# 64 unused bytes ahead of three groups of SBUF tiles in a one-core encoder block

## The chip, the cores and the metric

The kernel runs on one core of a Trainium2 chip. The metric is the device time of one execution in microseconds (us); before the change it is 1456.45 us, the median of three runs (1454.12, 1456.45 and 1457.32). Profiles are of one execution each; a profile's span runs from its first to its last instruction. TensorE does the matrix products, VectorE (DVE) and ScalarE (ACT) the elementwise work, GpSimd (POOL) some of it and a few transfers, SyncE (SP) issues most transfers.

## The reference, cut to what matters

One layer of a block over 1024 tokens of width 1024, all in float32. Two branches share one input projection:

```python
h = rms_norm(h_res, norm_w[layer])
z = jnp.einsum('bsd,dc->bsc', h, w_in[layer].astype(f32))
qkv_a, g_a, q_b, zf_fwd, zf_bwd, i_b, g_b, zgate_a, zgate_b = jnp.split(z, split_points, axis=-1)
...
q = rms_norm(qkv_a[:, :, g, 0], q_norm_w[layer, g])
k = rms_norm(qkv_a[:, :, g, 1], k_norm_w[layer, g])
...
y_a = jnp.einsum('bsc,cd->bsd', o_a.reshape(B, S, ATTN_WIDTH) * jax.nn.silu(g_a), w_proj_a[layer].astype(f32))
...
y_b = jnp.einsum('bsc,cd->bsd', o_b.reshape(B, S, HG_WIDTH), w_proj_b[layer].astype(f32))
merged = jax.nn.sigmoid(zgate_a) * y_a + jax.nn.sigmoid(zgate_b) * y_b
h_res = h_res + jnp.einsum('bsd,de->bse', merged, w_out[layer].astype(f32))
```

Branch (A) is dilated window attention in three groups of eight heads, branch (B) a gated linear recurrence (HGRN2) in both directions. Three places matter here: the input projection and its norm (the opening), the norms of q and k over the 64 columns of each head (the norm sums), and the last three products y_a, y_b and the output (the closing stage).

## The kernel before

**Products of split pairs.** [...] To keep precision, each operand is split into a high part and a low part, for weights `whi` and `wlo`, and each product is made of three matmuls: high by high, high by low, low by high. Nearly all such matmuls are of 128 by 128 (the stationary operand, loaded first) by 512 columns (the moving operand). In the names of the profile, `gp<-xh,whi` is a matmul into a tile `gp` with `xh` moving and `whi` stationary.

**The order of the work** is made while the program is built. The class `Plan` (from line 116) keeps a model of each engine's time, and `Builder.task` and `tick` (from line 247) put the work of ACT, DVE, POOL and SP between the products according to it. The model knows no addresses. Each engine then works through its own list in order.

**The stages on TensorE**, by the profile's times:

- *The opening* (from 6 us): the values of the first attention group are computed from `uhi`, `ulo` (the input times the norm's weight, split) before the norm is known (`u_products`, line 944), and those of the second group partly so (`u_group`, line 1031). The u tiles are stationary there, in part of it; the other part, and the third group's value pass (line 1107), uses the normalised input hT as stationary operand, in four quarters `hh00`, `hh01`, `hh10`, `hh11` and their low parts (line 727). The names leave the digits out: `hh`, `hl`. The quarter for tokens 512 and up and the first half of the width, `hh10` and `hl10`, lies in a pool of its own (line 721).
- *The blocks* (about 142 to 682 us): attention's q and k and other columns of the projection (`run_quads`, line 448), with a scheme of seven products in place of eight. Banks are called `qA`, `qE`, `qC`; the moving operands are hT and its sums `S0` to `S3`, the weights are stationary. For the norms of q and k, the squares are summed over each head by a matmul with a matrix of ones, `headones`, as stationary operand and the squares' parts `nhi`, `nlo` as moving ones (`head_sums`, line 1142). There are 48 such pairs of matmuls, called `nss`, put in between the others. The weights of this stage are loaded into the ring `qraw`; the finished q and k leave from the ring `ny`.
- *Attention, merge and HGRN2* (about 682 to 1248 us). In the merge, bursts of three matmuls called `al` spread the heads' weights (line 1532), with `sel` stationary and `alB` moving.
- *The closing stage* (from 1248 us to the end): first y_a (bank `gp`, moving `xh`, `xl`: the split output of attention), then y_b by seven products (banks `sA`, `sE`; moving `xh`, `xl`), then the output by seven products, in which `xh` and `xl` are stationary and the weights move (`seven`, line 2141). Weights come through the ring `eraw` and, for y_a, through `raw`; the gates come through the ring `sg`; evacuations go to `acc`, `ma` and `sg`.

**Where tiles lie.** A pool is a stretch of each partition of SBUF, and tiles lie in it one behind the other in the order in which they are first asked for. Pools that are closed make room for later ones. Three pools matter: `pre` (line 739, the opening), `blocks` (line 1095, in `blocks_start`) and `end` (line 1990, in `end_start`). Two earlier pools already hold unused tiles (`tinyPad`, line 631, and `pad`, line 708). The start of each tile, modulo 256 bytes, in the built program of before:

| tiles | pool | begins at, modulo 256 |
|---|---|---|
| raw, whi, wlo, stage | wts, stg | 224 |
| hh, hl, quarters 00, 01, 11; S0 to S3; hbh, hbl; sel, alB | hT, sums, h10b, merge | 224 |
| hh10, hl10 | h10 | 160 |
| uhi, ulo, x, v | pre | 160 |
| headones, qraw, spare, ny, nhi, nlo | blocks | 160 |
| acc, xh, xl, sg | end | 160 |
| eraw, ma, ob | endo | 224 |

Slices that the matmuls take of a tile begin at multiples of 512 bytes in it, so the start of each operand has its tile's remainder.

Of the kernel before, what the change touches and what calls it, by code (L numbers as in the profile page):

```python
# [8 lines left out]
F32 = mybir.dt.float32  # L9
# [613 lines left out]
def hybrid_block(ctx, tc, a, out):  # L623
# [115 lines left out]
    pre = pctx.enter_context(tc.tile_pool(name="pre", bufs=1))  # L739
# [2 lines left out]
    ones = pre.tile([128, 128], F32, name="ones")  # L742
    g_.memset(ones, 1.0)
    A0, A1 = 64, 576
    uhi = pre.tile([128, 8, 512], F32R, name="uhi")
    ulo = pre.tile([128, 8, 512], F32R, name="ulo")
    v_ring = b.ring(pre, "v", 10, [128, 512])
# [340 lines left out]
    def blocks_start():  # L1088

        if "p" in blk or blk["n"] < 16:  # L1090
            return
        b.low = "pool"
        tctx.close()
        a21.close()
        blk["p"] = p = gctx.enter_context(tc.tile_pool(name="blocks", bufs=1))
        blk["raw"] = b.ring(p, "qraw", QRAW, [128, 512])
        blk["spare"] = b.ring(p, "spare", SPARE, [128, 512])
        blk["ones"] = p.tile([128, 128], F32R, name="headones")
        blk["lo"] = b.ring(p, "nlo", 2, [128, 512], F32R)
        blk["hi"] = b.ring(p, "nhi", 2, [128, 512], F32R)  # L1100
        blk["y"] = b.ring(p, "ny", 4, [128, 512])
        a_.preload_act_table_set("natural_log_exp_and_others")
        v_.tensor_copy(blk["ones"].rearrange("p (j c) -> p j c", j=2),
                       half_ones[:, :, None].to_broadcast([128, 2, 64]))
        b.start_quads(blk["raw"])

    for g in (1, 2):
        if g == 2:
            grs = [tok_group(pos, 128 * i, evac_v(g, 128 * i), last=(k >= 6))
                   for k, i in enumerate((4, 5, 6, 7, 0, 1, 2, 3))]  # L1110
        for k, gr in enumerate(grs[:6]):
            if g == 1 and k < 5:
                continue
            b.run_unit([gr])
            if g == 2 and k >= 3:
                blocks_start()
        b.run_unit(grs[6:])
        pos += 8
    b.until(lambda: blocks_start() or "p" in blk)


# [866 lines left out]
    def end_start():  # L1988
        bctx.close()
        ectx["ep"] = ep = ctx.enter_context(tc.tile_pool(name="end", bufs=1))  # L1990
        ectx["acc"] = b.ring(ep, "acc", 10, [128, 512])
        ectx["xh"] = b.ring(ep, "xh", 12, [128, 512], F32R)
        ectx["xl"] = b.ring(ep, "xl", 12, [128, 512], F32R)
        ectx["sg"] = b.ring(ep, "sg", 5, [128, 512])
        for k in range(8):
            b.task("sp", [oaD], lambda k=k: load_oa(k % 4, k // 4), 4, ectx["acc"].soon)

    def load_oa(j, half):
        t = ectx["acc"].get()
        s_.dma_start(t, oaD[j, half])  # L2000
        b.task("act", [t], lambda: (OA.__setitem__((j, half), split_x(t)), ectx["acc"].done(t)), 4)
# [11 lines left out]
    for j in range(LATE, 8):  # L2013
        for half in range(2):
            b.run_unit([T_group(pos, half, evac_sg(1, j, half), half == 1)])
            if not ectx and all(st.get("f", 0) == 2 for st in H.values()):
                end_start()
        pos += 2
    b.drain()
    if not ectx:  # L2020
        end_start()
        b.drain()
# [7 lines left out]
    ep, acc, sgr = ectx["ep"], ectx["acc"], ectx["sg"]  # L2030
# [377 lines left out]
def _build(arrays):  # L2408
    import concourse.bacc as _bacc
    nc = _bacc.Bacc("TRN2", target_bir_lowering=False, num_devices=1)  # L2410
    args = {n: nc.dram_tensor(f"in_{n}_dram", v.shape, mybir.dt.from_np(v.dtype), kind="ExternalInput").ap()
            for n, v in arrays.items()}
    out = nc.dram_tensor("out_0_dram", (S, D), F32, kind="ExternalOutput").ap()
    with tile.TileContext(nc) as tc:
        hybrid_block(tc, args, out)
    return nc
# [9 lines left out]
```

## Time and profile before

| | |
|---|---|
| time, median of three runs | 1456.45 us |
| the three runs | 1454.12, 1456.45, 1457.32 us |
| span of the profiled execution | 1453.1 us |
| TensorE busy | 1444.3 us, 99% |
| DVE, ACT, POOL busy | 67%, 62%, 23% |
| instructions in the profile | 22946 |

The profiled execution's own time is not given apart from its span; the three timed runs lie 1.0 to 4.2 us above that span. [...] The chain of waits names, for each stretch of time, what the end of the program waited for.

### The profile page before, as it was taken

To read this page: it belongs to the slowest core of one execution; us is meant where nothing else is said; L and a number is where in the kernel's file an instruction comes from. 1 tells how busy PE (TensorE), PEld (TensorE's weight loads), DVE (VectorE), ACT (ScalarE), POOL (GpSimd) and SP (SyncE) were. 2 spreads that over 40 slices of the span, in tenths; PEclk is the share of its full clock that TensorE was granted. 3 is DMA by queue.
4 is the path that set the end of the run, shared out by engine and by line. 5 is a ranking of instruction groups with operands and counts; after the bars stand their busy time and mean duration, and the time that the engine had idled before them with its cause. 6 is when DMAs were issued, how large, how long until landed. Compare 5 with 4: busy or idle time off the path is not lost.

```text
span 1453.1 us, 22946 instructions
## 1 busy us (share of the span) xinstructions
PE 1444.3 (99%) x7930; PEld 1197.2 (82%) x7930; DVE 968.1 (67%) x1901; ACT 894.9 (62%) x1900; POOL 340.3 (23%) x356
## 2 busy tenths in 40 slices
PE   9999999999999999999999999999999999999998
PEld 8788888888888888888888778888888888788887
DVE  6673678678685788331564649487878786358973
ACT  7743767466565676443688852497777784558461
POOL 0102434464523433333002000031222221001011
PEclk9999999999999999999999999999999999999999
DMA  7746567777643334324848449354444453778665
GB/s 238 181 143 196 165 195 162 192 153 170 148 123 102 98 105 114 111 102 144 280 144 282 151 118 326 123 141 105 126 109 125 110 138 75 225 240 220 181 154 136
DMA packets 194992, 230.75 MB, mean 159 GB/s; under 512 B 46083, under 2 KB 118043, under 8 KB 194364
## 3 DMA queue, kind: packets, MB, share of 16 engines
q1 hardware_dynamic: 180188, 203.93, 45.0%
q0 software_dynamic: 13824, 25.17, 11.7%
q8 instruction: 62, 1.02, 0.3%
q14 instruction: 54, 0.44, 0.1%
q10 hardware_dynamic: 864, 0.19, 0.1%
HBM read 169.29 MB, written 81.43 MB: 173 GB/s over the span
## 4 chain that ended last, share of the span: by engine, by line
PE 90%; DVE 5%; ACT 3%; DMA 1%; issue 1%; SPq 0%; POOL 0%; ACTq 0%; DVEq 0%
PE gp L58 25%; PE qA L58 20%; PE qE L58 10%; PE sA L58 6%; PE qC L58 5%; PE sE L58 5%; PE u L58 3%; PE o L58 3%; PE oB L58 3%; PE pT L58 2%; PE sc L58 2%; PE nss L58 2%; DVE Bc L58 1%; PE U L58 1%; DVE S L58 1%
## 5 line engine op out<-in xcount | busy, mean ns | idle before, releaser
L58 POOL TENSOR_TENSOR wlo<-qraw,whi 128x512 fp32r<-128x512 f32 x135 | 194.3, 1444 | 381.8 <-ACT whi L58 293.8
L58 ACT ACTIVATE whi<-qraw 128x512 fp32r<-128x512 f32 x189 | 117.7, 626 | 100.8 <-DVE qraw L58 43.1
L58 DVE TENSOR_TENSOR qraw<-qraw,qraw 128x512 f32<-128x512 f32 x108 | 100.0, 927 | 39.0 <-POOL wlo L58 28.0
L58 PE MATMUL gp<-hh,whi 128*128 128x512 f32 x264 | 109.7, 416 | 0.0
L58 PE MATMUL gp<-hh,wlo 128*128 128x512 f32 x264 | 103.6, 393 | 0.0
L58 PE MATMUL gp<-hl,whi 128*128 128x512 f32 x264 | 103.0, 390 | 0.0
L58 ACT ACTIVATE as<-as,neg 128x192 f32<-128x192 f32 (+2 forms) x192 | 83.8, 442 | 16.8 <-DVE neg L58 16.7
L58 ACT ACTIVATE whi<-raw 128x512 fp32r<-128x512 f32 x92 | 57.6, 627 | 43.8 <-PE gp L58 18.7
L58 PE MATMUL qA<-hh,whi 128*128 128x512 f32 x216 | 84.4, 391 | 0.0
L58 PE MATMUL qA<-hh,wlo 128*128 128x512 f32 x216 | 84.3, 390 | 0.0
L58 DVE CUSTOM_DVE_ANT_0 as<-sc,abias 128x192 f32<-128x192 f32 (+2 forms) x192 | 56.0, 348 | 42.4 <-PE sc L58 27.1
L58 PE MATMUL qA<-hl,whi 128*128 128x512 f32 x216 | 84.0, 389 | 0.0
L58 POOL COPY mm<-Bc 128x8 f32<-128x8 f32 x64 | 32.2, 534 | 205.6 <-DVE Bc L58 123.6
L58 PE MATMUL gp<-whi,hh 128*128 128x512 f32 x192 | 78.6, 409 | 0.0
L58 PE MATMUL gp<-wlo,hh 128*128 128x512 f32 x192 | 75.2, 391 | 0.4 <-DVE wlo L58 0.4
L58 PE MATMUL gp<-whi,hl 128*128 128x512 f32 x192 | 75.0, 391 | 0.0
L58 DVE TENSOR_TENSOR wlo<-qraw,whi 128x512 fp32r<-128x512 f32 x54 | 37.3, 691 | 49.6 <-ACT whi L58 49.6
L58 DVE SCALAR_TENSOR_TENSOR ny<-ny,spare 128x512 f32<-128x512 f32 x48 | 67.4, 1405 | 1.6
L58 ACT ACTIVATE ny<-ny 128x512 f32<-128x512 f32 x96 | 60.8, 633 | 4.0 <-DVE ny L58 0.8
L58 PEld LDWEIGHTS gp<-hh,wlo 128*128 128x128 f32 x264 | 49.5, 188 | 11.0
L58 POOL DMA_DIRECT2D wlo<-in_w_in_dram x36 | 31.5, 875 | 113.6 <-ACT wlo L58 97.8
L58 PEld LDWEIGHTS gp<-hh,whi 128*128 128x128 f32 x264 | 49.8, 188 | 8.3
(306 smaller groups left out, 4208.2 us busy)
## 6 DMA issues: line engine op xcount, KB each, us to landing
qraw<-in_w_in_dram SPq DMA_DIRECT2D x108, 256.0 KB, 3.8
raw<-in_w_in_dram SPq DMA_DIRECT2D x84, 256.0 KB, 3.7
qkD<-ny SPq DMA_DIRECT2D x48, 256.0 KB, 2.8
wlo<-in_w_in_dram POOLq DMA_DIRECT2D x36, 256.0 KB, 4.4
sg<-sgD SPq DMA_DIRECT2D x32, 256.0 KB, 3.7
eraw<-wsD SPq DMA_DIRECT2D x32, 256.0 KB, 3.3
sgD<-stage SPq DMA_DIRECT2D x26, 256.0 KB, 2.7
ak<-qkD SPq DMA_DIRECT2D x6, 1024.0 KB, 6.6
```

What stands on the lines that cost most here:

```text
L58: got = f(*args, **kw)
```

## The change

Each of the three pools gets one more tile of 128 partitions by 16 float32 values, 64 bytes per partition, that nothing writes or reads. It is asked for ahead of the others (in `pre` behind `warm` and `ones`), so that all tiles behind it lie 64 bytes further.

```diff
     A0, A1 = 64, 576
+    pre.tile([128, 16], F32, name="prePad")
     uhi = pre.tile([128, 8, 512], F32R, name="uhi")
...
         blk["p"] = p = gctx.enter_context(tc.tile_pool(name="blocks", bufs=1))
+        p.tile([128, 16], F32, name="blkPad")
         blk["raw"] = b.ring(p, "qraw", QRAW, [128, 512])
...
         ectx["ep"] = ep = ctx.enter_context(tc.tile_pool(name="end", bufs=1))
+        ep.tile([128, 16], F32, name="endPad")
         ectx["acc"] = b.ring(ep, "acc", 10, [128, 512])
```

In the built programs, every engine's list holds the same instructions with the same waits in the same order; only addresses differ. Of the 5268 matmuls in the split form, these are the remainders of (moving, stationary) operand starts:

| moving, stationary | before | changed |
|---|---|---|
| 224, 224 | 4032 | 5184 |
| 224, 160 | 612 | 84 |
| 160, 224 | 528 | 0 |
| 160, 160 | 96 | 0 |

The 84 that are left read `hh10` or `hl10`. The other products (attention's scores, transposes, most of HGRN2, in plain float32) keep their addresses.

## The prediction

> **What bounds the kernel now.** I read the page first, then the granted clock, the waits of TensorE, the chain of waits in order of time, and last the timeline of single matmuls.
>
> ```profile
> span 1453.1 us, 22946 instructions
> PE   1444.3 (99%) x7930; PEld 1197.2 (82%) x7930; DVE 968.1 (67%) x1901; ACT 894.9 (62%) x1900; POOL 340.3 (23%) x356
> PE 90%; DVE 5%; ACT 3%; DMA 1%; issue 1%; SPq 0%; POOL 0%; ACTq 0%; DVEq 0%
> ```
> ```profile
> core 0: 1453.1 us, clock 1.000
> ```
> TensorE is busy for 99% of the span, 90% of the chain that ended last runs over it, and its clock was granted in full. So what a matmul takes counts nearly one to one, and differences in pace are not the clock's. Does TensorE wait in the closing stage? These are its only waits from 1240 us to the end:
>
> ```profile
> PE gp L58 <- ACT xh L58: 0.4, 1, 0.4
> PE gp L58 <- DVE xl L58: 0.2, 1, 0.2
> ```
> 0.6 us in 213 us, both at the stage's start. Behind that, every microsecond is matmul issue. Now the pace, in the chain of waits in order of time (start, length, what, how many):
>
> ```profile
> 915.50 40.81 PE gp L58 x180
> ...
> 1316.49 11.20 PE sA L58 x48
> ...
> 1394.48 21.97 PE sE L58 x96
> ...
> 1438.43 11.00 PE sA L58 x48
> ```
> All are matmuls of 128x128 by 512 in the same type. At 915 us both operands begin at 224 modulo 256: 40.81/180 = 226.7 ns each. At 1316 us the moving operand is at 160 and the stationary one at 224: 11.20/48 = 233.3 ns. From 1372 us the roles are swapped (moving 224, stationary 160): (21.97+11.00)/144 = 229.0 ns. Nothing waits in any of these stretches, so the start address is a candidate.
>
> Is it the address, or the stage? The trace holds a test. In the third value pass the stationary operand is hT, whose quarter h10 lies at 160 and whose other quarters lie at 224. One output tile uses 12 matmuls with the first and then 12 with the second, same weights' ring, same bank. Timeline of TensorE, first matmul of each dozen:
>
> ```profile
> 104.49 0.39 PE L58 MATMUL gp<-whi,hh 128*128 128x512 f32 x1
> ...
> 107.24 0.39 PE L58 MATMUL gp<-whi,hh 128*128 128x512 f32 x1
> ...
> 109.96 0.39 PE L58 MATMUL gp<-whi,hh 128*128 128x512 f32 x1
> ```
> The dozen at 160 took 2.75 us (229.2 ns each), the dozen at 224 took 2.72 us (226.7 ns): the closing stage's 229.0 again, inside one unit of work. That is my main reason to blame the address.
>
> **The change part by part.** It adds no instruction, wait or transfer, and no engine's order changes; it moves tiles by 64 bytes. So there is nothing to pay in issue, and the terms are counts of matmuls times differences of pace, all on TensorE's path. The counts, from the groups of instructions:
>
> ```profile
> L58 PE MATMUL gp<-xh,whi 128*128 128x512 f32 x64 | 25.4, 397 | 0.4 <-ACT xh L58 0.4
> L58 PE MATMUL sA<-xh,whi 128*128 128x512 f32 x64 | 25.3, 396 | 0.0
> L58 PE MATMUL sE<-xh,whi 128*128 128x512 f32 x48 | 19.0, 396 | 0.0
> L58 PE MATMUL sA<-whi,xh 128*128 128x512 f32 x64 | 24.8, 388 | 0.0
> L58 PE MATMUL sE<-whi,xh 128*128 128x512 f32 x48 | 18.6, 388 | 0.0
> L58 PE MATMUL gp<-whi,uhi 128*128 128x512 f32 x32 | 12.7, 395 | 0.0
> L58 PE MATMUL u<-whi,uhi 128*128 128x512 f32 x32 | 9.4, 401 | 0.0
> ```
> The name first behind the arrow is the moving operand. Each row stands for one of the three products of a split pair, so each count is taken three times.
>
> *Closing, x moving* (endPad): 3 x (64+64+48) = 528 matmuls from 233.3 to 226.7 ns: 528 x 6.6 = 3.5 us.
>
> *Closing, x stationary* (endPad): 3 x (64+48) = 336 matmuls from 229.0 to 226.7 ns: 0.75 us.
>
> *Opening* (prePad): 3 x 64 = 192 matmuls with uhi or ulo stationary. Their pace, from two starts 24 matmuls apart:
>
> ```profile
> 68.90 0.39 PE L58 MATMUL gp<-whi,uhi 128*128 128x512 f32 x1
> ...
> 74.39 0.39 PE L58 MATMUL gp<-whi,uhi 128*128 128x512 f32 x1
> ```
> 5.49/24 = 228.8 ns, so 192 x 2.1 = 0.4 us.
>
> *Norm sums* (blkPad): the 48 pairs of head sums are only 96 matmuls. But they disturb those behind them: the rows below are the first matmul of the dozen ahead of a pair, the pair, and the matmul 14 places on.
>
> ```profile
> L58 PE MATMUL nss<-nhi,headones 128*128 128x512 f32 x48 | 18.8, 391 | 0.0
> ```
> ```profile
> 162.19 0.39 PE L58 MATMUL qA<-hh,whi 128*128 128x512 f32 x1
> ...
> 164.91 0.39 PE L58 MATMUL nss<-nhi,headones 128*128 128x512 f32 x1
> ...
> 168.13 0.39 PE L58 MATMUL qA<-S1h,whi 128*128 128x512 f32 x1
> ```
> The dozen ahead took 2.72 us; the pair and the dozen behind it took 3.22 us where 14 x 226.7 = 3.17: 0.046 us lost per pair, 48 x 0.046 = 2.2 us. Would aligned sums still disturb? The merge stage's spreads (al) are bursts of three with other operands, between the same kind of neighbours, and both their operands are at 224:
>
> ```profile
> 881.50 0.68 PE al L58 x3
> 882.18 5.44 PE gp L58 x24
> 887.62 0.68 PE al L58 x3
> ```
> The burst takes 3 x 226.7, the 24 behind it 5.44 = 24 x 226.7. No disturbance. So the bounds are 0 (every switch disturbs) and 2.2 us; the aligned case is nearest to al, and I take 2.2.
>
> Sum: 3.5 + 0.75 + 0.4 + 2.2 = 6.8 us. The span would go from 1453.1 to 1446.3 us. The three timed runs are 1454.1, 1456.45 and 1457.3, that is 1.0 to 4.2 us above the profiled span; what lies around the span isn't touched. 1456.45 - 6.8 = **1449.6 us**.
>
> *What is late next.* A faster TensorE could run into its feeders. The tightest place that I found in the closing stage is where the second product of seven starts (engines DVE, SP, ACT, TensorE):
>
> ```profile
> 1294.13 0.69 DVE L58 TENSOR_TENSOR ma<-gp,sg 128x512 f32<-128x512 f32 x1 [2.11 <-PE gp L58]
> ```
> ```profile
> 1294.89 0.32 SPq L58 DMA_DIRECT2D sg<-sgD  x1
> ...
> 1297.62 2.05 SPq L58 DMA_DIRECT2D eraw<-in_w_proj_b_dram  x4
> ```
> ```profile
> 1304.05 0.68 DVE L58 TENSOR_TENSOR wlo<-eraw,whi 128x512 fp32r<-128x512 f32 x1
> ```
> ```profile
> 1305.60 0.39 PE L58 MATMUL sE<-xh,wlo 128*128 128x512 f32 x1
> ```
> The low part of the weights is ready at 1304.73 and first read at 1305.60: 0.87 us to spare. Its load stands in SP's queue behind an sg load that waits for a slot, which the evacuation of the last gp product frees: this chain starts from TensorE, so it moves forward with it. Against it TensorE gains only the 48 matmuls in between, 48 x 6.6 = 0.32 us. 0.55 us are left, so no stall in the sum; if all leads there vanished, it would cost tenths, not microseconds.
>
> [...] In the DMA rows (KB each, median us to landing), raw and stage begin at 224, qraw and ny at 160:
>
> ```profile
> qraw<-in_w_in_dram SPq DMA_DIRECT2D x108, 256.0 KB, 3.8
> raw<-in_w_in_dram SPq DMA_DIRECT2D x84, 256.0 KB, 3.7
> qkD<-ny SPq DMA_DIRECT2D x48, 256.0 KB, 2.8
> ...
> sgD<-stage SPq DMA_DIRECT2D x26, 256.0 KB, 2.7
> ```
> The tiles at 224 land no later than those at 160, on loads or stores; I put 0 on the transfers. [...]
>
> **The rivals.** *Only the switch counts* (6%): a change of operand set disturbs whatever its address. For it: every nss pair is followed by the slow dozen. Against it: al. Then 2.2 us stay: gain 4.6, 1451.8 us.
>
> *The closing stage is fed too late* (4%): TensorE catches up with the loads and splits, and the 4.25 us of the closing are lost in waits. For it: the 0.87 us above. Against it: the chain there starts from TensorE. Gain 2.6, 1453.9 us.
>
> *The address is not the cause* (6%): pace goes with the tiles' roles or neighbours, and nothing changes: 1456.45 us. For it: x operands are always the slow ones. Against it: the two dozens at 104 us. [...]
>
> *Slower* (4%): operands that share one phase with the tiles that ACT and DVE are writing (whi, wlo, xh, xl would then all be at 224) could collide on every read. Place: the 864 closing matmuls, now at (528 x 233.3 + 336 x 229.0)/864 = 231.6 ns on average, which is the point from which it loses. The slowest pace above is 233.3; if all 864 went as far above 233.3 as that is above 226.7 (239.9 ns), the closing would lose 864 x 8.3 = 7.2 us and, with 2.6 us gained elsewhere, the kernel would take 1461.0 us. Against it: at 915 us whi, wlo and hT share the phase and run at 226.7.
>
> **How the numbers follow.** My forecast has 80%, the rivals 6, 4, 6 and 4%. The range goes from the forecast less what the fastest run lies below the median (1456.45 - 1454.1 = 2.3): 1447.3; to the first rival plus what the slowest lies above it (0.9): 1452.7. That leaves out the other three rivals, 14%, and a few per cent of scatter. A measurement of this kernel can tell about 0.2%, 2.9 us, from no change. Faster by more: forecast and first rival, 0.86. Within it: late feeding and no effect, 0.10. Slower: 0.04.
>
> **What would show it.** In the chain of the changed kernel, sA and sE by 48 should read 10.88 us in both halves of the closing (48 x 226.7), the dozens behind nss 2.72, 24 opening matmuls 5.44; the third pass should still show its dozen at 2.75, since h10 stays at 160. The prediction is wrong if sA stays at 11.20 (address not the cause), if TensorE's waits from 1240 us grow above 1 us (late feeding), or if all of these come true and the time still does not fall by some 7 us.

## The result, and the profile after

The changed kernel takes 1449.05 us, the median of five runs (1447.51 to 1449.93); the kernel before took 1456.04 us in five runs beside them (1454.12 to 1457.32). The medians are 7.0 us apart; the ratio is 0.9957, with a 95% interval of 0.9946 to 0.9968, which is 4.7 to 7.9 us. The forecast was 1449.6 us in a range of 1447.3 to 1452.7.

The page of the changed kernel's profile, for the rows that were read first before:

```profile
span 1447.5 us, 22946 instructions
PE 1437.9 (99%) x7930; PEld 1197.1 (83%) x7930; DVE 967.6 (67%) x1901; ACT 894.9 (62%) x1900; POOL 338.8 (23%) x356
```
The same instructions; TensorE is busy 6.4 us less, DVE and ACT as long as before. TensorE still sets the time, and what it does got faster.

The chain of waits (start, length, what, how many) at the places where the prediction looked. The first rows lie around two pairs of norm sums, the row at 914 us is the stretch that served as a measure, the others are the closing stage with x moving, then with x stationary:

```profile
159.48 2.72 PE qE L58 x12
162.20 2.72 PE qA L58 x12
164.92 0.45 PE nss L58 x2
165.37 2.72 PE qE L58 x12
...
914.30 42.16 PE gp L58 x186
...
1345.94 10.88 PE sE L58 x48
...
1389.46 21.76 PE sE L58 x96
...
1432.98 10.89 PE sA L58 x48
```
48 matmuls of the closing stage take 10.88 us in both halves (10.89 in the last row), where 11.20 and 11.00 stood: 226.7 ns each, the pace of 914 us (42.16/186). A matmul's own row lasts 0.39 us and overlaps with the next one's, so a pace is a piece's length over its count, or the distance between starts. The dozen behind a pair of norm sums, at 165.37, takes 2.72 us like the one at 162.20. Before, the same pair and the two dozens behind it read:

```profile
165.07 0.46 PE nss L58 x2
165.53 2.76 PE qE L58 x12
168.30 2.72 PE qA L58 x12
```
Of the dozens that stand as pieces of their own between 140 and 690 us, 47 took 2.76 us before; none does now.

The timeline of TensorE, first the opening's matmuls 24 apart, then the first matmuls of two dozens of the third pass:

```profile
68.88 0.39 PE L58 MATMUL gp<-whi,uhi 128*128 128x512 f32 x1
74.32 0.39 PE L58 MATMUL gp<-whi,uhi 128*128 128x512 f32 x1
...
109.85 0.39 PE L58 MATMUL gp<-whi,hh 128*128 128x512 f32 x1
112.60 0.39 PE L58 MATMUL gp<-whi,hh 128*128 128x512 f32 x1
```
The 24 take 5.44 us (5.49 before). The dozen that reads hh10, which stayed at 160, takes 2.75 us as before.

Where in the program was the time gained? The last matmul of the blocks, then the first and the last of the closing stage, before:

```profile
680.47 0.39 PE L58 MATMUL qA<-hh,wlo 128*128 128x512 f32 x1
...
1247.95 0.39 PE L58 MATMUL gp<-xh,whi 128*128 128x512 f32 x1
...
1449.02 0.40 PE L58 MATMUL sA<-whi,xl 128*128 128x512 f32 x1
```
and after:

```profile
678.16 0.39 PE L58 MATMUL qA<-hh,wlo 128*128 128x512 f32 x1
...
1246.72 0.39 PE L58 MATMUL gp<-xh,whi 128*128 128x512 f32 x1
...
1443.48 0.39 PE L58 MATMUL sA<-whi,xl 128*128 128x512 f32 x1
```
Of 5.54 us at the last matmul, 1.23 were there when the closing stage began, so the closing stage gained 4.31: 4.25 was forecast. Up to there 2.6 were forecast, and more than 1.23 had been gained at one time: the blocks ended 2.31 us earlier. Some 1.1 us went again behind them. TensorE's waits between 660 and 880 us have one where attention begins that is not in the list of before:

```profile
PE sc L58 <- issue: 1.5, 1, 1.5
```
The profiles of the experiments below have a wait before `sc` too, from 0.7 to 2.1 us, also where only `endPad`, far behind it, was added; only the one profile of before lacks it. So these two profiles, whose spans differ by 5.6 us, show less than the change is worth, and the medians, 7.0 us apart, are the better measure. What makes this wait come and go was not tested.

### The profile page after: what moved, and what is told of

It is laid out like the page before. It is cut to its first block, busy times and chain, and to the rows that moved or that the text cites. A ratio compares the mean times of both kernels' runs of the same rounds, so it can differ in the third digit from the quotient of the medians.

```text
span 1447.5 us, 22946 instructions
## 1 busy us (share of the span) xinstructions
PE 1437.9 (99%) x7930; PEld 1197.1 (83%) x7930; DVE 967.6 (67%) x1901; ACT 894.9 (62%) x1900; POOL 338.8 (23%) x356
## 4 chain that ended last, share of the span: by engine, by line
PE 89%; DVE 6%; ACT 3%; issue 1%; DMA 1%; POOL 0%; SPq 0%; DVEq 0%
PE gp L58 27%; PE qA L58 20%; PE qE L58 10%; PE qC L58 5%; PE sA L58 5%; PE sE L58 4%; PE u L58 3%; PE oB L58 3%; PE o L58 3%; PE pT L58 2%; PE sc L58 2%; PE nss L58 2%; DVE Bc L58 1%; PE U L58 1%; DVE S L58 1%; DVE xs L58 1%
## 5 line engine op out<-in xcount | busy, mean ns | idle before, releaser
L58 DVE SCALAR_TENSOR_TENSOR ny<-ny,spare 128x512 f32<-128x512 f32 x48 | 63.2, 1316 | 1.6
L58 ACT ACTIVATE stage<-gp 128x512 f32<-128x512 f32 x39 | 22.9, 591 | 54.9 <-PE gp L58 39.7
```

Of the source, the lines that this page charges most:

```text
L58: got = f(*args, **kw)
```

## The experiments

The theory at the start: matmuls in the split form run at 226.7 ns when both operands begin at the same place modulo 256, and slower otherwise, and each of the three pads is worth the sum of its matmuls. The rivals were that something other than the start sets the pace, and that a start at 224 is good in itself. The diffs below show each kernel's edits against the kernel before, and all times are set beside runs of that kernel on the same chip.

**One pad at a time.** First `endPad` alone:

```diff
+        ep.tile([128, 16], F32, name="endPad")
```


> Only the tile ahead of the end pool stays. If the operands' start sets the pace: the closing stage's sA and sE take 10.88 us per 48 in both halves, gain 528 x 6.6 + 336 x 2.2 ns = 4.2 us (1451.8 us beside 1456.0); the dozens behind nss stay at 2.76 us. If the stage's roles set it: sA stays at 11.20 us and the time does not move. If feeding takes the gain back: sA at 10.88 but TensorE waits of about 4 us in the closing stage.

Measured: 1451.27 us (five runs, 1449.98 to 1451.95) beside 1455.84 (21 runs), ratio 0.9966 (0.9954 to 0.9979): 4.6 us less. Its chain:

```profile
159.38 2.76 PE qE L58 x12
162.14 2.72 PE qA L58 x12
...
1304.40 10.88 PE sE L58 x48
...
1391.44 21.76 PE sE L58 x96
```
The closing stage is at 226.7 ns in both halves; the dozen behind the norm sums is still slow.

Then `blkPad` alone:

```diff
+        p.tile([128, 16], F32, name="blkPad")
```


> Only the tile ahead of the blocks pool stays. If aligned sums do not disturb their neighbours: all dozens behind nss at 2.72 us, gain 2.2 us (1453.8 us beside 1456.0), closing stage as before (11.20 and 11.00 us per 48). If the switch of operands disturbs whatever its address: dozens at 2.76 us and no gain.

Measured: 1454.12 us (11 runs, 1451.28 to 1455.22), ratio 0.9984 (0.9975 to 0.9993): 1.7 us less.

```profile
159.82 2.72 PE qE L58 x12
162.54 2.72 PE qA L58 x12
...
1314.89 11.20 PE sA L58 x48
...
1392.88 21.97 PE sE L58 x96
```
The mirror image: the dozen behind the norm sums is undisturbed, the closing stage as before. So a change of operand set cost nothing by itself (2.72 us for the dozen behind the pair, as for those with no pair ahead); it cost 0.04 us (2.76 in the kernel before) where the sets differed in their starts. The pairs had equal remainders before as well (both operands at 160): what differed was the pair's start from the 224 of the matmuls around it. The pad also moved `qraw`, `spare` and `ny`, which no matmul reads; that the pairs did it is read from the place of the slow dozens, right behind them.

And `prePad` alone:

```diff
+    pre.tile([128, 16], F32, name="prePad")
```


> Only the tile ahead of uhi stays. By the pace: 24 opening matmuls in 5.44 us instead of 5.49, gain 0.2 to 0.4 us, too little for the timing to tell from none. If other things in the opening hang on these starts, the time moves by more than 1 us.

Measured: 1455.59 us (11 runs), ratio 0.9999 (0.9990 to 1.0008). Two starts 24 matmuls apart in the opening:

```profile
68.70 0.39 PE L58 MATMUL gp<-whi,uhi 128*128 128x512 f32 x1
...
74.14 0.39 PE L58 MATMUL gp<-whi,uhi 128*128 128x512 f32 x1
```
5.44 us, the pace of 226.7 ns, but 0.25 us in the medians is less than this measurement can tell. The three together, 4.57 + 1.72 + 0.25 = 6.5 us, are the whole change's 7.0 within what the runs scatter. No part works against another.

**The last quarter too.** If the rule holds, `hh10` at 224 should run its dozens at 2.72 as well. `prePad` is replaced by a pad ahead of `hh10`, which moves `uhi`, `ulo` behind it along, so that all 5268 matmuls of the split form have both operands at 224:

```diff
+    a21pool.tile([128, 16], F32, name="h10Pad")
...
+        p.tile([128, 16], F32, name="blkPad")
...
+        ep.tile([128, 16], F32, name="endPad")
```


> The opening's tile is moved ahead of h10 instead (the pool below), so that hh10 and hl10 begin at 224 too and all 5268 split matmuls are at (224, 224); blocks and end as in the change. If start sets the pace: the dozens of the third value pass all take 2.72 us, and the time is the changed kernel's 1449.05 less 84 x 2.3 ns = 0.2 us, 1448.9 us. If the changed kernel's gain needed h10 at 160 or came from elsewhere: clearly above 1449.05 us.

Measured: 1449.01 us (five runs, 1447.76 to 1450.74), ratio 0.9950 (0.9937 to 0.9964). That is the changed kernel's time: the 84 matmuls are worth 84 x 2.3 ns = 0.2 us, which is lost in the scatter. By the distances of starts, all dozens that read `hh10` come down, from 2.75 to 2.72 us (one to 2.73). Its profile shows something else, the feeding of the closing stage. The chain around the place that the prediction named as the tightest:

```profile
1294.04 4.91 DMA ob<-obD
...
1299.05 0.70 DVE acc L58
...
1303.04 0.69 DVE wlo L58
...
1303.78 10.72 PE sE L58 x46
1314.51 10.88 PE sA L58 x48
1325.38 11.09 PE sE L58 x48
```
The low part of the weights is written until 1303.73, and the matmul that reads it starts at 1303.78: the lead is gone. The piece has 46 matmuls, not 48, because the chain reaches the first two through other work, and the sE piece at 1325 takes 0.21 us more than its 10.88. DVE came to wlo late because acc stood ahead of it and waited for the load of ob; the weights' own load was not the last.

**Is 224 good in itself?** Three kernels have `endPad` alone in other sizes, with x at 32, 96 and 192 while the weights stay at 224:

```diff
+        ep.tile([128, 32], F32, name="endPad")
```


> 128 bytes ahead of the end pool, nothing else: x begins at 32 modulo 256 and the weights stay at 224. Equal remainders count, any difference costs the same: closing as in before, 233.3 ns with x moving and 229.0 ns with x stationary. The size of the difference counts: another pair of numbers, under or over these. Only 224 is fast, whatever stands beside it: also slow, so that this run alone does not tell it from the first.

```diff
+        ep.tile([128, 48], F32, name="endPad")
```


> 192 bytes ahead of the end pool: x at 96, weights at 224, the largest distance of 128 bytes. Any difference costs the same: 233.3 and 229.0 ns. [...]

```diff
+        ep.tile([128, 8], F32, name="endPad")
```


> 32 bytes ahead of the end pool: x at 192, weights at 224. Any difference costs the same: 233.3 and 229.0 ns. If steps of 64 bytes count and what is below them does not (192 and 224 lie in the same 64): 226.7 ns in both halves.

And one has the three pads as in the changed kernel (not shown in the diff), but 64 bytes less in an earlier pool, which puts weights and x both at 160 while hT and its sums stay at 224:

```diff
-    consts.tile([128, 48], F32, name="pad")
+    consts.tile([128, 32], F32, name="pad")
```


> The changed kernel with the older unused tile ahead of the weights cut by 64 bytes: weights and everything on their side of SBUF begin 64 bytes earlier, so that in the closing stage both operands are at 160, and in the blocks the stationary weights are at 160 beside moving hT and S at 224. Equal remainders count: closing at 226.7 ns in both halves as in the changed kernel, blocks at 229.0 ns instead of 226.7 (2268 matmuls, some 5 us more), other products with hT slower too, so the whole takes some 10 us longer than the changed kernel. Only 224 is fast: closing over 229 ns in both halves.

Measured in one run each: 1453.97, 1456.41, 1458.02 and 1458.36 us, beside 1454.41 of the kernel before. One run can be 3 us off (the lowest of the 11 with `blkPad` alone lies 2.8 us below their median), so the chains decide. With x at 32:

```profile
1315.18 10.99 PE sA L58 x48
...
1392.52 22.40 PE sE L58 x96
```
with x at 96:

```profile
1317.12 11.15 PE sA L58 x48
...
1395.19 22.31 PE sE L58 x96
```
with x at 192:

```profile
1318.18 11.20 PE sA L58 x48
...
1396.58 22.40 PE sE L58 x96
```
and with weights and x at 160, the blocks first:

```profile
163.78 2.75 PE qA L58 x12
166.53 0.47 PE nss L58 x2
...
923.19 36.86 PE gp L58 x161
...
1322.26 10.88 PE sA L58 x48
...
1398.51 21.76 PE sE L58 x96
```
The last one settles it. The closing stage, with both operands at 160, runs at 226.7 ns, as it did with both at 224 in the changed kernel: 224 is not good in itself, nor 160 bad. The blocks and the stretch at 923 us, whose moving operand stayed at 224 while the weights went to 160, now run at 2.75/12 = 229.2 and 36.86/161 = 228.9 ns, where 226.7 stood. The whole takes 9 us more than the changed kernel's 1449.05, where some 10 were expected. With x at 32 the two halves have changed places: 229.0 ns with x moving, 233.3 with x stationary. All chains together, by the start of the moving operand less that of the stationary one, modulo 256 bytes:

| moving less stationary | pace, ns | seen with (moving, stationary) |
|---|---|---|
| 0 | 226.7 | (224, 224), (160, 160) |
| +64 | 228.9 to 229.2 | (224, 160), (32, 224) |
| -64 | 233.3 | (160, 224), (224, 32) |
| +128 or -128 | 232.4 | (96, 224), (224, 96) |
| +32, -32 | 233.3 | (224, 192), (192, 224) |

The pads move other tiles along (`acc` and `sg` in the closing stage), but the same difference gives the same pace beside quite different tiles, in the closing stage, the blocks and the third pass. So neither "any difference costs the same" nor "steps below 64 bytes do not count" holds. Two readings of the traces bear out 256 bytes as the period: a difference of 128 is not free (232.4 ns), and in the kernel with all split products at 224, where 72 of the 5268 matmuls have starts that differ by 256 modulo 512, 60 of these in an undisturbed row, from 81.70 to 95.30 us, run at 13.60/60 = 226.7 ns like the others.

**Does the rule reach the plain float32 products?** HGRN2's, attention's and the transposes' products are mostly 128 columns wide or narrower, and many have operands with different remainders. In one more kernel pads in their pools bring their operands to equal remainders, on top of the kernel with all split products at 224; beside it ran the changed kernel once more:

```diff
+    consts.tile([128, 8], F32, name="identPad")
-    consts.tile([128, 48], F32, name="pad")
+    consts.tile([128, 40], F32, name="pad")
...
+    a21pool.tile([128, 16], F32, name="h10Pad")
...
+        p.tile([128, 16], F32, name="blkPad")
...
+        ap.tile([128, 16], F32, name="attnPad")
...
+    hp.tile([128, 40], F32, name="skPad")
...
+    hp.tile([128, 32], F32, name="igPad")
...
-        t = hp.tile([128, 8], F32, tag="Gt", name=b.name("Gt"), bufs=2)
+        t = hp.tile([128, 32], F32, tag="Gt", name=b.name("Gt"), bufs=2)
...
+        ep.tile([128, 16], F32, name="endPad")
```


> Unused bytes also ahead of h10, ident, attention's tiles, sk, ig and (in a wider scratch tile) kT, so that the plain float32 products of attention and HGRN2 have equal remainders too, as the split ones have. If the rule of equal remainders holds for plain float32 products: kT, U and oB come 109 ns apart instead of 109 to 112, some 600 records by up to 3 ns, and the split matmuls behind each burst of them are not slowed (1.8 us from 960 to 1250 us in the changed kernel): 2 to 4 us below the changed kernel. If plain products are indifferent and the slow split ones come from the switch between the two forms: 0.2 us below it, from h10 alone.

> The changed kernel once more, on the same chip beside the other one: 0.9957 of before within its interval, 1449 us.

Measured: 1449.05 us (five runs, 1448.69 to 1449.76), ratio 0.9955 (0.9940 to 0.9969), and for the changed kernel 1449.85 (1447.03 to 1450.49), ratio 0.9954 (0.9941 to 0.9968). No gain beyond the changed kernel, which is the second of the two cases expected. Two groups of plain products, in the changed kernel with differences of +64 (oB) and 128 (kT):

```profile
L58 PE MATMUL oB<-S,qr 128*128 128x128 f32 x224 | 35.9, 277 | 1.1 <-DVE S L58 0.8
L58 PE MATMUL kT<-ident,sk 128*128 128x128 f32 x112 | 16.9, 272 | 0.0
```
and in the kernel with all remainders equal:

```profile
L58 PE MATMUL oB<-S,qr 128*128 128x128 f32 x224 | 35.9, 277 | 1.1 <-DVE S L58 0.7
L58 PE MATMUL kT<-ident,sk 128*128 128x128 f32 x112 | 16.9, 272 | 0.0
```
Busy time and mean are the same to the last digit, and so are the distances between starts, 111.7 ns for oB in both kernels and 108.6 and 108.7 for kT. The form of the theory that took in every matmul falls: these products showed no effect of where their operands start. Whether that is due to the plain float32 form or to the 128 columns was not separated.

## Why the prediction was right, point by point

- *The mechanism*: right, and the first rival (only the switch counts), the third (not the address) and the fourth (a shared phase collides) are refuted: by `blkPad` alone, whose switches became free (the dozens behind them at 2.72 us instead of 2.76); by `endPad` alone, which changed the closing stage and left the norm sums' dozens slow; and by 10.88 us wherever starts were shared, at 224 or at 160. Nor are starts at multiples of 32 bytes all alike: they ran at four different paces here, 226.7, 228.9 to 229.2, 232.4 and 233.3 ns.
- *Closing, x moving*: forecast 3.5 us. Summed over the distances of starts in the two traces, the 528 matmuls went from 124.38 to 120.83 us, 3.55. Both sums hold waits of about the same size, 1.18 us before (all at the stage's start) and 1.07 after (0.61 there, 0.46 in the feeding below), so that the agreement to 0.05 us is partly luck; the pace itself is the 11.20 and 10.88 us of 48 matmuls.
- *Closing, x stationary*: forecast 0.75; 76.69 to 75.93 us over the 335 distances between 336 matmuls, 0.76.
- *Norm sums*: forecast 2.2; the blocks' 2364 matmuls went from 538.04 to 535.84 us, 2.20. The choice of the upper bound, by the rows of `al`, was right; between 0 and 2.2 the profile of before had no nearer row.
- *Opening*: forecast 0.4; measured 0.1 in these two profiles. The 96 matmuls into `gp` went from 22.18 to 21.99 us. The 96 into `u` were at 22.27 and are at 22.33: past the first two they went from 229.0 to 227.1 ns, which is 0.2 us, but the first two distances of starts, which hold the wait at the stage's start, were 0.51 and 0.23 us and are 0.59 and 0.39. That is not the pad's doing: with `blkPad` alone they are 0.59 and 0.43. The pace was forecast rightly, and this wait took half of the term back.
- *Feeding*: forecast that 0.55 us of lead stay and that no stall comes; this part did not hold. One half of its sum was right: from the evacuation of the last gp product (ma) to the matmul that reads wlo, TensorE took 11.47 us before and 11.13 after, 0.34 less, where 0.32 was forecast. But the load that sets when DVE writes wlo is the one of ob, which stands in SP's queue behind the same sg load, and the prediction followed the one of eraw. From the issue of those loads to acc 4.8 us passed before, and 5.3, 5.1, 5.5 and 4.7 in the two profiles of the changed kernel and the two with all split products at 224; their leads are 0.06, 0.28, 0.06 and 0.61 us. In the changed kernel's first profile more is lost at a second place, which the prediction did not look at. Its chain there goes through a load of sg and a late xl:

```profile
1318.43 4.10 DMA sg<-sgD
...
1325.41 0.70 DVE xl L58
...
1326.16 8.91 PE sE L58 x38
```
The matmuls at this place lose 0.35 us. From 1260 us on, distances of starts above 250 ns exceed the pace by nothing before, and in these four by 0.46, 0.17, 0.48 and 0.00 us. (Waits at the stage's start, around 1250 us, are not counted: 0.6 us and more in every kernel, with or without `endPad`.) So "tenths, not microseconds" held, and the second rival appears with about a tenth of its price.
- *Transfers at zero*: the loads of sg, whose tiles moved from 160 to 224, land in a median of 3.7 us before and 3.4 after, the stores of acc in 2.0 and 2.1. No chain of the changed kernel names a wait for a load of weights or a store that the one of before lacks; the loads of ob and sg that it does name are those above. A price of a transfer's start by itself was not measured.
- *The sum*: 3.55 + 0.76 + 2.20 + 0.13 = 6.6 us on TensorE by the measured terms where 6.8 were forecast, and 7.0 by the medians. The profile of before stood lower than its kernel's median (time and span are 1.8 us apart in every run that lists both, so it took about 1454.9 us), so the forecast was rightly subtracted from the median and not from the span.

## What to carry to other kernels

Where TensorE is the bound, as here at 99% busy, and runs long rows of wide matmuls in the split form (F32R in the code), lay both operands of a matmul out so that they begin at the same place modulo 256 bytes: that ran at 226.7 ns here, and the other differences that were tried at 228.9 to 233.3. A pad of 16 floats ahead of a pool was worth up to 2.8% of such a stretch here (11.20 to 10.88 us). Read it off the chain of waits: divide undisturbed pieces of the same shape by their counts, and if stages differ with nothing waiting, compare the addresses. Align the kinds that alternate, too, since a pair of matmuls at another start slowed the dozen behind it from 2.72 to 2.76 us.

## What the runs showed of the hardware that was not expected

- In these runs the pace went with the difference of the two starts and with its sign: 64 bytes one way cost 2.3 ns per matmul, 64 the other way 6.6 ns, 128 cost 5.7, and 32 either way 6.6. What in TensorE makes it so is not visible in the traces, and stays open.
- Two matmuls at another start, each with equal remainders itself, made the twelve behind them 0.04 us slower, though those were aligned among themselves. The loss is a passing one with a form of its own: behind the pair at 165 us in the kernel before, the distances of starts from the third matmul on are 233, 236, 224, 231, 236, 228, 233 and 230 ns, and then 227 again. The same series stands in the aligned opening of the changed kernel from 6.88 us, behind a wait (233, 236, 224, 231, 236, 228, 233, 231), and its beginning behind bursts of the narrow plain products, in the kernel with everything aligned too (230, 233, 236, 224 from 1009.14 us); behind such bursts it costs some 1.8 us of TensorE between 960 and 1250 us of the changed kernel. So a pair at another start left the same series as a break in the row of matmuls. Why it took the row some ten matmuls to settle stays open, and nothing was tried against it.
- Plain float32 products of 128 columns did not react to such differences: 111.7 ns between starts at +64 and at 0, 108.6 and 108.7 ns at 128 and at 0.
